# Two decoder layers on one core: the turns of the mixers' three chains in another order

## The chip, the cores and the metric

The kernel runs on one core of a Trainium2 chip. The metric is device microseconds of one execution. Five engines work side by side, each in the order of its own queue: PE (matrix products and transposes), DVE (VectorE), ACT (ScalarE), POOL (GpSimd) and SP, which here issues DMAs. A wait between engines is a wait for a semaphore.

## The reference

Two layers of a hybrid decoder trunk run on 512 tokens of width 1024, in f32. Each layer is a SwiGLU block, a token mixing block, a second SwiGLU block and a gated embedding, each with a norm ahead and a norm behind. The change touches only token mixing:

```
h = pre(x) @ W_in, columns split into attention | mLSTM | RWKV-7
y_attn  = sliding_window_gqa(q, k, v, sinks)            # 8 query heads, blocks of 128 queries x 256 keys
y_mlstm = sigmoid(o_m) * norm(mlstm_chunkwise(q, k, v, i, f))   # 4 heads, a running state from chunk to chunk
y_rwkv  = norm(rwkv7_scan(r, decay, k, v, a, b)) * gate         # 4 heads, a running state from token to token
x = x + post(concat(y_attn, y_mlstm, y_rwkv) @ W_out)
```

`o_m` is itself a projection of `h`: 1024 columns in, 256 out.

## The kernel before

Weights and activations of the large products are split into a high and a low part, and each product is three matmuls (`mm3`, lines 169 to 171). ACT makes the high part of a weight (line 141), DVE or POOL the low part (line 142).

In `mix` the inputs of all three mixers are projected first, RWKV's score matrices are made, and then `weave` runs four chains in turns. Each chain is a Python generator, and one call of `run` lets it record its instructions up to its next `yield`. The chains are:

- **A**, attention: 8 units (a block of 128 queries times a group of 4 heads), in 9 turns. A unit makes the scores (`pS`, line 1337), their maximum on DVE (1341, 1343), the exponentials on ACT (1349), sums and scaling on DVE and POOL (1350 to 1356), transposes (`pT`, 1366) and the product with the values (`po`, 1372). The product of unit u is recorded after the scores of unit u+1.
- **R**, RWKV: `rwkv_solve` inverts triangular blocks in two halves (`pt0`, `pgi`, `pt1`, `pz`, line 1017, with DVE additions at 1027 to 1034; then `pwt`, 869, and `pzq`, 877). The first half takes 15 turns. `rwkv_scan` then makes 8 steps, each dependent on the state `st` of the one before (`pq` 909, DVE 913, `pst` 919 to 921, state 923 and 925, output `py` 929 to 932); the turns of the second half of the solve lie between the first four steps. After the fifth and the last step come a norm (956 to 961, with a power on POOL at 179) and the transposes and gate products of `rwkv_back` (`pyt` 968, `pgf` 972, DVE 976 and 977).
- **M**, mLSTM: 4 chunks of 128 tokens. A chunk makes a weight matrix (`pwt` 1149, exponentials 1154, mask on POOL 1156), products `pss` (1163), `pnum` (1176), `pint` (1182), a state update from `pc` (1195), then norm and gating (1210 to 1223, the power at 179 and the multiplication by the gate `ng` at 1223 on POOL) and, in its `back`, the transposes `pym` (1140). All its products go through two PSUM banks in turn.
- **P**, the output gate projection of mLSTM: `tm_proj` into `pog`, 96 matmuls that need only `xh`, `xl` and two weight blocks, then a sigmoid on ACT and a product with the norm's gain on POOL (`ng`, 1123 and 1124).

The string `PLAN` gives the order of the turns; a letter whose chain is done is skipped, and what is left at its end runs in the order A, P, R, M. Two rules bind it. M doesn't start before A has had 7 turns. And the mixers' output is written over `xh` and `xl`, which P reads: a turn of R or M that would write there first runs P to its end, and attention's output `yt` is split into `xh` and `xl` once A and P are both done.

The recorded order isn't the order in the queues. The program is built with a scheduler that takes instructions by readiness on its own model of time and by recorded order, so a change of `PLAN` moves instructions on every engine, and it settles in which order tiles get their buffers.

Behind `weave` come `out_proj` (products `y`, lines 169 to 171, with weights `wo` for the first half of the columns and `wot` for the second), whose first half splits its weights on POOL, and the FFN. The second half's weights lie in the storage that the mixers used, so their loads `wor` wait until that is free. Lines named here and in the profile are those of the kernel before; in the changed kernel every line behind `PLAN` has a number that is lower by one.

Of the kernel before, what the change touches and what calls it, by code (L numbers as in the profile page):

```python
# [36 lines left out]
OE = "0000"  # L37
END = "XN"
NFL = {1: 1, 2: NT}
PLAN = ("AAAPAAAAAAAAAAAAAAPRARPARPAARRAPPAPA"  # L40
        "RRPARRPRRRMMMMARRPRRARPRARMRAAAPRMAR")
for _n, _w in (("amask", 384), ("mk_m", 64), ("mk_n", 256), ("mk_r", 64), ("m1", 64), ("m2", 64), ("bones", 128),
               ("triu", 128), ("lmask", 128), ("sel", 128)):
    CONSTS[_n] = (NCONST, _w)
# [28 lines left out]
class Trunk:  # L73
# [579 lines left out]
    def weave(self, l):  # L653
# [9 lines left out]
        def run(c):  # L663
            if c in done:
                return
            if c in "RM" and held.pop(c, None) and "P" not in done:
                while "P" not in done:
                    run("P")
            while c == "M" and c not in cycles and "A" not in done and count["A"] < 7:
                run("A")  # L670
            count[c] += 1
            if c not in cycles:
                self.lanes(*lanes[c])
            else:
                self.main, self.aux, self.chain = cycles[c]
            r = next(chains[c], "end")
            cycles[c] = self.main, self.aux, self.chain
            if r == "back":
                held[c] = True
            if r == "end":  # L680
                done.add(c)
            if c in "AP" and "A" in done and "P" in done:
                for t, y in enumerate(self.ys):
                    ts = slice(t * 128, (t + 1) * 128)
                    self.split(self.yh[:, 0:4, ts], self.yl[:, 0:4, ts], y.rearrange("p (a i) -> p a i", a=4),
                               self.pl_(1))
                done.add("Y")

        for c in PLAN:
            run(c)  # L690
# [828 lines left out]
```

## Time and profile before

| | us |
|---|---|
| median of three runs | 2180.99 (2180.17 to 2182.21) |
| the profiled run | 2184.07 |
| its span | 2182.4 |
| PE busy | 2104.1 (96%) |
| DVE busy | 1719.7 (79%) |
| ACT busy | 1008.8 (46%) |
| POOL busy | 327.4 (15%) |

The profile is of one execution. PE is busy nearly all the time, but ends of matmuls are modelled, so a row of dependent small matmuls also shows as busy. Layer 1 is a repetition of layer 0, and its mixing stage comes 1081.9 us later.

### The profile page before, as it was taken

What the parts mean: (1) busy time and instruction counts of PE and PEld (TensorE: products, weight loads), DVE (VectorE), ACT (ScalarE), POOL (GpSimd) and SP (SyncE); (2) the same over time, 40 slices, a digit from 0 to 9 for tenths busy, and PEclk for the clock granted to TensorE, in tenths of its full rate; (3) what the DMA queues carried; (4) which work ended last, traced back from release to release, by engine and by line L of the source; (5) the groups of instructions that cost most, each with busy time, mean ns of one, the idle gap of its engine ahead of it and who ended that gap; (6) DMA issues with size and microseconds to landing.
All of it is one profiled execution on the core that took longest, in us unless ns stands there. A gap on an engine that the chain in (4) does not pass through costs nothing.

```text
span 2182.4 us, 39847 instructions
## 1 busy us (share of the span) xinstructions
PE 2104.1 (96%) x16256; PEld 1957.1 (90%) x16256; DVE 1719.7 (79%) x2886; ACT 1008.8 (46%) x1653; POOL 327.4 (15%) x424
## 2 busy tenths in 40 slices
PE   6999999999988999999979999999999989999998
PEld 6999999898767999999869999998887789999996
DVE  8999977655768999977689999775457689999774
ACT  5444434446545444434554444345465454444343
POOL 5000011032234000011330000110412330000121
PEclk9999999999999999999999999999999999999999
DMA  4223224321041222224313222242220413222241
GB/s 174 106 99 115 69 78 156 119 64 55 21 154 40 108 106 101 84 68 175 105 59 116 105 90 88 81 175 87 64 64 2 155 59 117 97 97 78 78 143 71
DMA packets 69799, 208.62 MB, mean 96 GB/s; under 512 B 15984, under 2 KB 17008, under 8 KB 69616
## 3 DMA queue, kind: packets, MB, share of 16 engines
q1 hardware_dynamic: 69328, 205.55, 27.0%
q8 instruction: 128, 2.10, 0.4%
q10 hardware_dynamic: 288, 0.52, 0.1%
q14 instruction: 55, 0.45, 0.1%
HBM read 199.23 MB, written 6.82 MB: 94 GB/s over the span
## 4 chain that ended last, share of the span: by engine, by line
PE 82%; DVE 8%; ACT 4%; DMA 2%; issue 2%; POOL 1%; SPq 0%; POOLq 0%; DVEq 0%; ACTq 0%
PE y L465 18%; PE p L170 13%; PE p L169 13%; PE p L171 13%; PE pkrv L171 1%; PE pkrv L170 1%; PE pkrv L169 1%; PE y L169 1%; PE y L170 1%; PE y L171 1%; DMA ws_r<-in_w_ffn_out 1%; DVE w L142 1%; PE pgt L171 1%; PE pgt L169 1%; PE pgt L170 1%
## 5 line engine op out<-in xcount | busy, mean ns | idle before, releaser
L171 PE MATMUL p<-xh,w 128*128 128x256 f32 x1408 | 399.6, 285 | 6.3 <-POOL w L142 6.3
L169 PE MATMUL p<-xh,w 128*128 128x256 f32 x1408 | 400.1, 286 | 4.7 <-DVE gate L369 2.1
L170 PE MATMUL p<-xl,w 128*128 128x256 f32 x1408 | 400.3, 285 | 0.2 <-DVE xl L142 0.2
L169 PE MATMUL p<-tx,w 128*128 128x256 f32 x1056 | 296.9, 284 | 11.3 <-ACT tx L141 10.8
L170 PE MATMUL p<-tx,w 128*128 128x256 f32 x1056 | 296.3, 284 | 11.2 <-DVE tx L142 11.2
L171 PE MATMUL p<-tx,w 128*128 128x256 f32 x1056 | 295.7, 283 | 0.0
L171 PEld LDWEIGHTS p<-xh,w 128*128 128x128 f32 x1408 | 270.4, 192 | 7.0 <-POOL w L142 7.0
L169 PEld LDWEIGHTS p<-xh,w 128*128 128x128 f32 x1408 | 270.4, 193 | 6.9 <-DVE gate L369 2.9
L170 PEld LDWEIGHTS p<-xl,w 128*128 128x128 f32 x1408 | 270.9, 192 | 0.9 <-DVE xl L142 0.8
L141 ACT ACTIVATE w<-ws 128x1024 fp32r<-128x1024 f32 x176 | 185.9, 1056 | 153.4 <-PE p L171 134.8
L142 DVE TENSOR_TENSOR w<-ws,w 128x1024 fp32r<-128x1024 f32 x176 | 223.2, 1269 | 18.4 <-ACT w L141 17.2
L169 PEld LDWEIGHTS p<-tx,w 128*128 128x128 f32 x1056 | 202.5, 192 | 13.3 <-ACT tx L141 12.1
L170 PEld LDWEIGHTS p<-tx,w 128*128 128x128 f32 x1056 | 202.7, 192 | 12.1 <-DVE tx L142 12.1
L171 PEld LDWEIGHTS p<-tx,w 128*128 128x128 f32 x1056 | 201.4, 192 | 0.0
L141 ACT ACTIVATE w<-wr 128x512 fp32r<-128x512 f32 (+1 forms) x176 | 148.3, 844 | 114.5 <-PE p L171 67.1
L465 PE MATMUL y<-wo,hq 128*128 128x256 f32 x1536 | 193.3, 283 | 0.0
L465 PEld LDWEIGHTS y<-wo,hq 128*128 128x128 f32 x1536 | 186.4, 190 | 0.8
L501 POOL TENSOR_TENSOR tb<-tb,ln_ffn_post 128x512 f32<-128x512 f32 x16 | 24.1, 1530 | 1082.6 <-ACT junk L198 1082.6
L465 PE MATMUL y<-ws_r,h 128*128 128x256 f32 x672 | 158.3, 379 | 0.4 <-DMA ws_r<-in_w_ffn_out 0.2
L142 DVE TENSOR_TENSOR w<-wr,w 128x512 fp32r<-128x512 f32 (+1 forms) x161 | 150.9, 940 | 5.3 <-ACT w L141 4.9
L465 PEld LDWEIGHTS y<-ws_r,h 128*128 128x128 f32 x672 | 121.2, 189 | 14.9 <-DMA ws_r<-in_w_ffn_out 1.2
L357 DVE TENSOR_TENSOR ws<-wr 128x1024 f32<-128x1024 f32 x88 | 115.0, 1307 | 5.6 <-DMA wr<-in_w_ffn_in 5.3
(426 smaller groups left out, 4675.7 us busy)
## 6 DMA issues: line engine op xcount, KB each, us to landing
wr<-in_w_ffn_in SPq DMA_DIRECT2D x176, 512.0 KB, 4.1
ws_r<-in_w_ffn_out SPq DMA_DIRECT2D x56, 512.0 KB, 3.3
wo_r<-in_w_ffn_out SPq DMA_DIRECT2D x32, 512.0 KB, 3.3
pkrv_r<-in_w_rw SPq DMA_DIRECT2D x16, 512.0 KB, 3.5
wpg_r<-in_w_ple_gate SPq DMA_DIRECT2D x16, 512.0 KB, 4.5
xd<-x SPq DMA_DIRECT2D x8, 512.0 KB, 2.7
x<-xd SPq DMA_DIRECT2D x8, 512.0 KB, 3.4
pq_r<-in_w_q SPq DMA_DIRECT2D x8, 512.0 KB, 3.5
```

The costliest lines, as they stand in the source:

```text
L141: self.nc.scalar.activation(hi, src, AF.Copy)
L142: (eng or self.nc.vector).tensor_tensor(lo, src, hi.bitcast(F32), ALU.subtract)
L169: mm(out, a[0], b[0], start=first, stop=False)
L170: mm(out, a[0], b[1], start=False, stop=False)
L171: mm(out, a[1], b[0], start=False, stop=last)
L357: v_.tensor_tensor(sx.rearrange("p (i c) -> p i c", i=2), r[:, :, lo], r[:, 1].rearrange("p (i c) -> p i c", i=2), ALU.add)
L465: nc.tensor.matmul(banks[n][:, u], x, y, start=n not in seen, stop=last and i == len(todo) - 1, skip_group_check=True)
L501: (g_ if not h or QL[0] == "1" else v_).tensor_tensor(tb, tb, gain[:, h * 512:h * 512 + 512], ALU.mult)
```

## The change

Only `PLAN` is another string. The new one is written as repeated letters: A has its nine turns first, then R has the 15 turns of its first solve, then M its first turn, then R the first step of the scan, and only then P. R and M follow in turns.

```diff
-PLAN = ("AAAPAAAAAAAAAAAAAAPRARPARPAARRAPPAPA"
-        "RRPARRPRRRMMMMARRPRRARPRARMRAAAPRMAR")
+PLAN = 9 * "A" + 15 * "R" + "M" + 4 * "R" + "PM" + 4 * "R" + "M" + 3 * "R" + "PM" + 5 * "R" + "MM" + 5 * "R" + "MMM" + 4 * "R" + "MMM"
```

On PE, in layer 0, the gate projection's matmuls (`pog`) stood behind the transposes `pT` of attention's second unit, with the first solve's products (`pt`) and other products between them. Before:

```order
L1366 MATMUL pT<-ident,arena 128x128 x4
L169 MATMUL pog<-pog,xh 128x256
...
L1017 MATMUL pt_6077<-arena 64x64 x7
L1372 MATMUL po<-arena 64x512
...
L171 MATMUL pog<-pog,xl 128x256
L1091 MATMUL pir<-ident,vg 4x128 x4
```

In the changed kernel the first of them stands behind the second solve (`pzq`) and ahead of the very last attention product (`po`), and from the twelfth on they are one block up to the scan's fifth step (`pst`, `py`):

```order
L876 MATMUL pzq<-x,arena 64x64 x13
L908 MATMUL pq<-st,arena 64x128 x2
L918 MATMUL pst<-st,ident 64x128
L1371 MATMUL po<-arena 64x512
L168 MATMUL pog<-pog,xh 128x256
...
L170 MATMUL pog<-pog,xl 128x256
L920 MATMUL pst<-arena_4155 64x64 x2
```

The projection has moved from the third attention unit to the end of the eighth.

On ACT, in layer 0, the gates (`ng`) stood ahead of attention's units three to eight and of all of mLSTM. Before:

```order
L141 ACTIVATE xh<-yt 128x4x128
L1107 ACT_TABLE_LOAD
L1107 ACTIVATE vg<-vg 128x16
L141 ACTIVATE wo<-wo_r 128x1024
L1123 ACT_TABLE_LOAD
L1123 ACTIVATE ng<-pog 128x256 x4
L141 ACTIVATE wo<-wo_r 128x1024
L1112 ACT_TABLE_LOAD
```

In the changed kernel they stand, with the conversions of attention's output (`xh<-yt`) and of two weights (`wo`), ahead of the scan's state update (`st`), and mLSTM's third chunk (`pwt`, line 1153 here) comes two scan steps later:

```order
L140 ACTIVATE xh<-yt 128x4x128 x3
L140 ACTIVATE wo<-wo_r 128x1024
L1122 ACT_TABLE_LOAD
L1122 ACTIVATE ng<-pog 128x256 x4
L140 ACTIVATE wo<-wo_r 128x1024
L924 ACTIVATE st<-pst,pl 64x64 x2
L931 ACTIVATE x<-py 128x128 x2
L924 ACTIVATE st<-pst,pl 64x64 x2
L140 ACTIVATE xh<-arena 128x256 x2
```

The scan's updates are now queued behind the gates.

On PE, at the end of the weave in layer 0, mLSTM's last chunk (`pnum`, `pint`) was interleaved with the scan's last step. Before:

```order
L1176 MATMUL pnum<-vg,arena 128x128 x3
L1182 MATMUL pint<-arena 128x130 x2
L931 MATMUL py<-arena_4155 64x64 x2
L929 MATMUL py<-st,arena 64x128
L931 MATMUL py<-arena_4155 64x64 x2
L1140 MATMUL pym<-ident,mg 128x128 x2
L169 MATMUL y_6815<-wo,xh 128x512
```

In the changed kernel the third and the fourth chunk follow each other behind the scan, with RWKV's last transposes (`pyt`, `pgf`) between them:

```order
L1175 MATMUL pnum<-vg,arena 128x128 x4
L1181 MATMUL pint<-arena 128x130 x2
L1194 MATMUL pc<-vg,mg 128x130 x2
L1139 MATMUL pym<-ident,mg 128x128 x2
L967 MATMUL pyt<-ident,x 128x128 x4
L971 MATMUL pgf<-xg,arena 128x256 x2
L1148 MATMUL pwt<-ident,vg 128x128 x4
L1162 MATMUL pss<-arena 128x128 x4
L1175 MATMUL pnum<-vg,arena 128x128 x4
L1181 MATMUL pint<-arena 128x130 x2
L1139 MATMUL pym<-ident,mg 128x128 x2
```

Nothing but the first output products (`y`) stands behind them.

## Rows read from the trace of the kernel before

**Rows 1.** The page's chain of work that ended last, by engine

```profile
PE 82%; DVE 8%; ACT 4%; DMA 2%; issue 2%; POOL 1%; SPq 0%; POOLq 0%; DVEq 0%; ACTq 0%
```

**Rows 2.** Windows: length, then busy us (instructions) by engine, PEclk, DMA, GB/s

```profile
528.40:544.60 16.20, 16.08 (x135) 14.55 (x135) 7.77 (x25) 10.37 (x21) 1.67 (x2) 1.00 0.20 63
544.60:611.50 66.90, 63.83 (x777) 47.20 (x776) 49.25 (x162) 34.59 (x107) 19.50 (x21) 1.00 0.06 18
611.50:633.60 22.10, 16.78 (x131) 13.01 (x131) 17.30 (x50) 8.53 (x23) 8.77 (x7) 1.00 0.14 49
633.60:675.00 41.40, 41.40 (x189) 34.19 (x190) 23.74 (x27) 19.85 (x40) 15.27 (x16) 1.00 0.46 178
...
1693.40:1715.50 22.10, 16.77 (x131) 13.01 (x131) 17.30 (x50) 8.53 (x23) 8.78 (x7) 1.00 0.15 48
```

**Rows 3.** Timeline of PE: start, us, engine line op, names; the last attention product

```profile
610.01 1.45 PE L1372 MATMUL po<-arena 128*64 128x512 f32 x3
```

**Rows 4.** Timelines of four engines: mLSTM's last chunk up to its last transposes

```profile
614.66 1.14 ACT L1154 ACTIVATE arena<-pwt,vg 128x128 f32<-128x128 f32 x4 [0.81 <-PE pwt L1149]
615.93 0.64 POOL L1156 TENSOR_SCALAR_AFFINE_SELECT arena<-arena 128x512 f32<-128x512 f32 x1 [7.97 <-ACT arena L1154]
618.92 0.74 DVE L1164 SCALAR_TENSOR_TENSOR arena<-pss,arena 128x256 f32<-128x256 f32 x2
620.46 0.94 PE L1176 MATMUL pnum<-vg,arena 128*128 128x128 f32 x6
621.23 0.61 PE L1182 MATMUL pint<-arena 128*128 128x130 f32 x4
626.40 2.35 POOL L142 TENSOR_TENSOR wo<-wo_r,wo 128x1024 fp32r<-128x1024 f32 x1
633.56 0.44 PE L1140 MATMUL pym<-ident,mg 128*128 128x128 f32 x2 [1.51 <-POOL mg L1223]
```

**Rows 5.** Waits of PE from 490 to 650: the longest

```profile
PE pyt L968 <- DVE x L961: 2.0, 1, 2.0
```

**Rows 6.** Timeline of PE: two matmuls of the gate projection

```profile
544.19 0.28 PE L170 MATMUL pog<-pog,xh 128*128 128x256 f32 x1
544.31 0.28 PE L171 MATMUL pog<-pog,xl 128*128 128x256 f32 x1
```

**Rows 7.** Timelines of PE and ACT: one step of RWKV's scan and the next's start

```profile
616.49 0.44 PE L909 MATMUL pq<-st,arena 128*64 128x128 f32 x4
...
618.36 0.40 PE L931 MATMUL py<-arena 128*64 128x64 f32 x4
619.10 0.51 ACT L925 ACTIVATE st<-pst,pl 64x64 f32<-64x64 f32 x2
619.87 0.32 PE L909 MATMUL pq<-st,arena 128*64 128x128 f32 x1
```

**Rows 8.** Lines from 528 to 634: attention's exponentials; busy us, mean ns, idle before

```profile
L1349 ACT ACTIVATE arena<-arena,mx 128x256 f32<-128x256 f32 x24 | 11.9, 497 | 9.0 <-DVE mx L1343 7.0 <-DVE vg L1115 2.0
```

**Rows 9.** Timeline of ACT at the end of the gate projection

```profile
542.96 1.06 ACT L141 ACTIVATE wo<-wo_r 128x1024 fp32r<-128x1024 f32 x1 [0.25 <-PE pog L171]
544.03 1.28 ACT L1123 ACT_TABLE_LOAD   x1
545.33 1.21 ACT L1123 ACTIVATE ng<-pog 128x256 f32<-128x256 f32 x4
546.40 1.08 ACT L141 ACTIVATE wo<-wo_r 128x1024 fp32r<-128x1024 f32 x1
```

**Rows 10.** Timelines of DVE and POOL: a DVE instruction beside a weight split

```profile
549.65 1.53 DVE L1343 SCALAR_TENSOR_TENSOR mx<-mx,ns 128x4 f32<-128x4 f32 x1
548.79 2.37 POOL L142 TENSOR_TENSOR wo<-wo_r,wo 128x1024 fp32r<-128x1024 f32 x1
```

**Rows 11.** Windows at the start of the second FFN block, layer 0

```profile
695.00:700.00 5.00, 1.88 (x9) 1.48 (x9) 5.00 (x4) 3.08 (x6) 4.77 (x3) 0.74 0.00 0
700.00:705.00 5.00, 5.00 (x28) 5.00 (x28) 3.88 (x6) 0.00 (x0) 0.00 (x0) 0.58 0.00 0
```

## Prediction

> **What bounds the kernel now.** I read the chain of waits first: 82% of it is PE [rows 1], so the reader is to take PE as the engine that sets the time, and to ask of the change only where PE gains or loses a wait. Then the busy time by stretch, in the part of each layer in which the three mixers are woven [rows 2]. There are four stretches in layer 0. From 528.4 to 544.6 PE runs mLSTM's output gate projection, `pog`, among the other chains. From 544.6 to 611.5 the attention finishes while RWKV's second solve and scan and mLSTM's chunks run beside it; PE shows 63.83 of 66.90 us busy and DVE 49.25, so this stretch is dense. From 611.5 to 633.6 the attention is gone, only the scan's and mLSTM's dependent chains are left, and PE is busy 16.78 of 22.10 us. From 633.6 on the output projection has everything it needs and PE has no idle time in 41.40 us. The last attention product is the row at 610.01, ending at 611.46 [rows 3], and the last transpose of mLSTM's output, `pym`, starts at 633.56 [rows 4]. Layer 1 repeats this 1081.9 us later with the same figures (the tail's last row of [rows 2]: 16.77 of 22.10), so I work out one layer and double it. The waits by engine say what ends the idle time of that tail: PE waits longest for the DVE multiply before RWKV's transposes, 2.0 us [rows 5]. The tail is chains, not matmuls.
>
> **The change part by part.** No instruction's work is added or removed; the list of turns alone changes. What matters on PE is where the 96 `pog` matmuls stand, since they depend on nothing in the chains and can fill any gap.
>
> *The filler leaves the lead.* Two `pog` matmuls start 0.12 us apart (544.19 and 544.31 in [rows 6]), so the projection is worth 96 x 0.12 = 11.5 us of PE, which before is spread over the first of the four stretches. Now all of it stands behind the last but one attention product. More goes behind the last one: mLSTM's third chunk up to its `pint`, the first `pym` and the second half of the scan's fifth step. A scan step issues for 2.3 us on PE (616.49 to the end of the `py` row, 618.76, in [rows 7]), so its half is 1.2; the chunk's largest group, `pnum`, takes 0.94 for six of its eight rows [rows 4], and it has three more groups. I estimate 5 us in all. If PE waited no longer in the lead than it does now, the last attention product would end at 611.5 - 11.5 - 5 = 595.0.
>
> It will wait longer. In the new order of PE, RWKV's `pwt` products come right behind the first solve, and each needs the solve's last DVE addition. On DVE that stands behind the softmax of the fourth attention unit, which waits for that unit's four exponentials (497 ns each, [rows 8]); on ACT those now stand behind three table loads (1.28 us each, the form of the row at 544.03 in [rows 9]) instead of two. Nothing independent is left in PE's order there. I make that wait 5 us, of which the same stretch already has about 2 as waits between the chains, so I add 3, between -5 (the chains pack closer than they do now) and +8. Attention's end: 598.
>
> *The projection itself.* 11 of the 96 matmuls stand ahead of the last attention product, so 85 x 0.12 = 10.2 us follow: `pog` ends at 608.2. Call this E.
>
> *The tail behind it.* This is the term that decides. Before, ACT's run of conversions and gates at `pog`'s end (from 542.96: weight conversion 1.06, table load 1.28, gates 1.21, weight conversion 1.08, [rows 9]) held up nothing that was late. Now the scan's state update is queued behind the same run and one more conversion of attention's output: about 0.6 + 1.06 + 1.28 + 1.21 + 1.08 + 0.5 for the update itself = 5.7 us, so the sixth step starts at E + 6. A step takes 3.4 us from one `pq` to the next (616.49 to 619.87, [rows 7]); with RWKV's first back transform between, the eighth starts at E + 14. mLSTM's third chunk has its exponentials queued on ACT behind the seventh step's update and a table load: they end at E + 16.6 (1.28 + 1.14, [rows 4, 9]). From the exponentials to the end of `pint` I count mask, product, `pnum` and `pint`, 0.64 + 0.74 + 0.94 + 0.61, some 3.3 with hand-overs [rows 4]: E + 20. The fourth chunk's first transpose stands behind RWKV's last transposes, which wait for the norm of the eighth step: E + 23. Its exponentials and the same 3.3 us bring `pint` to E + 27.5. From there to the last `pym` it took 11.7 us before (621.84 to 633.56, [rows 4]), of which some 4 were POOL's weight split (2.35) and a DVE queue of RWKV's last step, which now comes earlier: I take 7.5. Sum E + 35; in layer 1 the order puts the third chunk's exponentials ahead of the scan's updates, which saves about 3. I take 34 for both, between 26 and 41. Below 22.1 it can't be, since all that the tail holds now stays in it.
>
> The last `pym` then starts at 608.2 + 34 = 642.2, against 633.6: 8.6 us a layer, 17 us for two.
>
> *Other engines and queues.* On POOL two `wo` splits and the four gate products now stand in the tail, ahead of the mask of mLSTM's third chunk; a split is 2.37 us [rows 10] and a gate product has a quarter of its elements, so 7 us is my estimate for the six. They begin at about E + 2 and are over by E + 10, and the mask is ready for POOL only at E + 16.6: the scan hides them, and if it did not, one split, 2.4 us, would be late. On SP the `ln_mix_post` loads move behind four loads of `w_out` and six of FFN weights. They are first read when the first output tile is done, 96 - 18 matmuls after the last `pym`; hidden, with nothing to gain. On ACT and DVE two splits of `w_out`'s second half move ahead of the split of the last `pym`, and three of PE's matmuls that read them ahead of the `pym` itself. That adds a wait for a DMA that can start only when the arena is free; behind it are 18 matmuls that don't read mLSTM's last tile. I cost it at 0, at most 3.
>
> The profiled run was 2184.07 us (span 2182.4) and the three timed runs have their median at 2180.99. The sum is a difference, so I add it to the median: 2181 + 17 = **2198 us**.
>
> **A page against the trace.** In [rows 10] a DVE instruction on 128x4 elements takes 1.53 us while POOL splits a weight, and ends when POOL does (551.18 and 551.16). The Trainium skill, "SBUF — State Buffer", section "Who interferes with whom", states that DVE and GpSimd have one port pair in common, which the first holds for a whole instruction when the DVE instruction reads two inputs from SBUF. The trace agrees, with the 1.53 us. By that rule the four DVE conversions of attention's output, all with two SBUF inputs and now beside POOL's splits and gates, would each wait, and the tail would be longer by up to two splits.
>
> **The rivals.**
>
> *The lead packs tighter (not slower).* Place: from 528 to the last attention product. With attention first in every turn, its units, the solve and mLSTM's first two chunks could fill PE without `pog`. For it: the dense stretch has DVE at only 49 of 67 us [rows 2], so there is room. Against it: with DVE and PE waiting on each other in order, less independent work means more waits. Its price: the lead 4 us better than now instead of 3 worse, and a tail of 30, gives 591 + 10.2 + 30 = 631.2, 2.4 us a layer to the good: 2176. It decides if `pog` ends before 599.6 with a tail of 34, or the tail is under 25.4 with the lead as forecast. Chance 0.17.
>
> *The waits only change places (no change).* The tail's extra waits equal those saved ahead of it, as PE has the same matmuls in all. 2181; chance 0.09, and 0.01 of the others falls there too. Against it: that needs a lead nearly free of waits.
>
> *PE's clock falls in the thin tail, or POOL blocks DVE there (slower still).* Place: E to E + 34. At the start of the FFN PE's busy time falls to 1.88 of 5 us, and the granted clock is 0.74 there and 0.58 in the next 5 us, when PE is busy throughout [rows 11]; of the two levels, 2.4 and 1.2 GHz, it has the lower for most of that time, and about 2 us of work are lost in 5. The tail has about 20 us of matmuls in 34. If the output projection starts at such a clock, 3 us a layer are lost, and one blocked split adds 2.4: 17 + 11, so 2209. Against it: 76% busy in the tail of before left the clock at 1.00 [rows 2]. Chance 0.10.
>
> **How the numbers follow.** The forecast has 0.64. From the bounds, a layer goes from 608.2 - 8 + 26 = 626.2 (7.4 us better) to 608.2 + 5 + 41 + 3 = 657 (23 us worse); both ends at once are unlikely. I leave out the outer part on each side: 2175 to 2215, the likeliest case's own range being 2188 to 2210. Within 0.2%, 4.4 us, a measurement can't tell a change. Faster 0.16, same 0.10, slower 0.74: the first rival is nearly all the chance of faster, the forecast and the last rival nearly all of slower.
>
> **What would show it.** Right: `pog` in one block of some 12 us that ends at 604 to 612 in layer 0; the last `pym` 30 us or more behind it, with PE under 70% busy between; a PE wait of some us at RWKV's `pwt` before the block; each layer 5 to 12 us longer and nothing changed after the output projection begins. Wrong: the block ends before 600, or mLSTM's third chunk runs under the scan in both layers and the tail is 27 us; or the FFN behind it, whose instructions the scheduler also orders a little differently, moves by more than 3 us.

## The result, and the profile after

The changed kernel takes 2215.23 us (median of four runs, 2213.61 to 2221.49) against 2181.49 (2180.17 to 2182.21) for the kernel before: a ratio of 1.0161, interval 1.0143 to 1.0179, 34 us slower. The forecast was 2198, slower by 17. The direction holds, the size is half of what came.

The chain of waits still has PE as the engine that sets the time, with 2 points less of it and 1 point more each for DVE and DMA than in [rows 1]:

```profile
PE 80%; DVE 9%; ACT 4%; DMA 3%; issue 2%; POOL 1%; SPq 0%; DVEq 0%; POOLq 0%; ACTq 0%
```

Windows of the changed kernel, columns as in [rows 2]: of layer 0 the lead (what stands ahead of `pog`), `pog` itself, the tail up to the last `pym`, the output projection; the fifth row is layer 1's tail.

```profile
528.40:595.60 67.20, 64.27 (x751) 46.52 (x750) 49.34 (x172) 35.30 (x107) 12.01 (x13) 0.95 0.05 16
595.60:608.60 13.00, 13.00 (x101) 11.90 (x102) 3.80 (x7) 4.84 (x7) 0.71 (x1) 1.00 0.01 1
608.60:648.20 39.60, 31.54 (x193) 26.15 (x193) 21.13 (x60) 15.68 (x38) 16.47 (x16) 0.74 0.30 102
648.20:689.60 41.40, 41.18 (x190) 33.83 (x188) 21.02 (x26) 18.10 (x39) 16.48 (x16) 1.00 0.35 133
...
1714.70:1750.10 35.40, 28.26 (x208) 21.82 (x208) 22.13 (x62) 15.06 (x36) 16.85 (x15) 0.90 0.31 109
```

`pog` is one block that ends at 608.6. Behind it come 39.6 us until the last `pym` where the kernel before had 22.1 behind its last attention product [rows 2], with a granted clock of 0.74 instead of 1.00. So for a part of that tail PE has the lower of its two levels, 1.2 GHz, and the tail's last chunk shows it: `pnum` takes 2.05 us for eight matmuls and `pint` 1.07 for four, where [rows 4] have 0.94 for six and 0.61 for four. Timelines of PE and DVE, changed kernel:

```profile
636.34 2.05 PE L1175 MATMUL pnum<-vg,arena 128*128 128x128 f32 x8 [1.84 <-DVE arena L1163]
638.18 1.07 PE L1181 MATMUL pint<-arena 128*128 128x130 f32 x4
642.95 1.43 DVE L1219 TENSOR_SCALAR ss<-ss 128x4 f32<-128x4 f32 x1
647.16 0.39 PE L170 MATMUL y<-wo,xl 128*128 128x512 f32 x1
647.38 0.87 PE L168 MATMUL y<-wot,xh 128*128 128x512 f32 x3
648.09 0.38 PE L1139 MATMUL pym<-ident,mg 128*128 128x128 f32 x2
```

The last `pym` doesn't wait for its `mg`, which ends at 646.73. From 641.00 on PE makes 21 products `y` of the output projection that stand ahead of it in PE's queue (the last four are the rows at 647.16 and 647.38), and the first of them start 0.43 us apart, the later ones 0.23: the lower level and the higher. So the tail ends with PE's own work and not with a bare chain.

The longest waits of PE from 528 to 650, the answer to [rows 5]. The first is in the lead, in the solve's second level and not at `pwt`, where the prediction put it; the second is the scan's sixth step behind ACT's run at the end of `pog`.

```profile
PE pz L1016 <- DVE arena L1026: 2.3, 1, 2.3
PE pq L908 <- ACT st L924: 1.9, 1, 1.9
PE pnum L1175 <- DVE arena L1163: 1.8, 1, 1.8
```

**Where the time came.** This profile's span is 2219.8 us, 37.4 more than before's 2182.4. Counted by where each stage begins, 13.6 us are there when FFN2 of layer 0 begins, 3.4 more when its products `p` end, 3.0 more between there and the end of layer 1's projections for the mixers, then again 13.6 in layer 1's mixing and 3.6 in its FFN2, and 0.2 at the end. The 3.0 are mostly what runs differ by: PE's order there is that of the kernel before, and in experiment 7, where it is so too, the same stretch was 2.0 us longer than in the profile of before. The output projection itself is no longer than before (41.4 us from the last `pym` to FFN2's first product, 42.3 before). So there are two places: the weave, 13.6 us a layer where 8.6 were forecast, and FFN2, 3.5 a layer where nothing was.

FFN2 first. PE there waits for `tx`, which DVE makes from the transposes of the last block. Timeline of DVE in the kernel before, at the start of FFN2:

```profile
683.26 3.50 DVE L209 SCALAR_TENSOR_TENSOR xn<-x,r,ln_ffn_pre 128x512 f32<-128x512 f32 x2
...
688.97 2.79 DVE L142 TENSOR_TENSOR w<-ws,w 128x1024 fp32r<-128x1024 f32 x1
691.68 0.68 DVE L241 TENSOR_TENSOR xr<-xr,xtp 128x512 f32<-128x512 f32 x1
692.28 1.21 DVE L357 TENSOR_TENSOR ws<-wr 128x1024 f32<-128x1024 f32 x1
693.42 0.68 DVE L242 SCALAR_TENSOR_TENSOR tx<-xtp,xr 128x512 f32<-128x512 f32 x1
694.02 0.68 DVE L243 TENSOR_TENSOR tx<-xtp,tx 128x512 f32<-128x512 f32 x1
```

and in the changed kernel:

```profile
698.18 4.58 DVE L208 SCALAR_TENSOR_TENSOR xn<-x,r,ln_ffn_pre 128x512 f32<-128x512 f32 x2
...
704.96 1.70 DVE L141 TENSOR_TENSOR w<-ws,w 128x1024 fp32r<-128x1024 f32 x1
706.70 1.22 DVE L356 TENSOR_TENSOR ws<-wr 128x1024 f32<-128x1024 f32 x1
707.84 1.22 DVE L141 TENSOR_TENSOR w<-ws,w 128x1024 fp32r<-128x1024 f32 x1
708.97 0.68 DVE L240 TENSOR_TENSOR xr<-xr,xtp 128x512 f32<-128x512 f32 x1
...
710.17 0.68 DVE L241 SCALAR_TENSOR_TENSOR tx<-xtp,xr 128x512 f32<-128x512 f32 x1
710.77 0.68 DVE L242 TENSOR_TENSOR tx<-xtp,tx 128x512 f32<-128x512 f32 x1
```

Before, `xr` follows one split of a weight; now a `ws` and a second split stand ahead of it. Counted from FFN2's first product (676.0 and 689.6), the second `tx` behind `xr` starts at 18.0 us before and 21.2 now: 3.2 us, nearly all of FFN2's 3.4 (241.3 us from its first product to its last before, 244.7 now). The instruction `xn` ahead of it has grown from 3.50 to 4.58 us; beside it POOL has another split, moved by the scheduler. A pair like it with no split on POOL takes 1.42 in the same trace (690.22). The Trainium skill, "SBUF — State Buffer", section "Who interferes with whom", says that a DVE instruction with two inputs from SBUF shares a port pair with a GpSimd instruction that reads SBUF, and that the one that came first keeps it; the trace agrees, with 4.58 against 1.42.

Windows at the start of FFN2, the answer to [rows 11]: PE is idle longer, and the stretch at the lower level comes behind it as before.

```profile
709.00:714.00 5.00, 1.16 (x2) 0.58 (x2) 5.00 (x7) 2.79 (x7) 3.61 (x3) 0.66 0.00 0
714.00:719.00 5.00, 2.84 (x13) 2.85 (x14) 4.41 (x5) 1.20 (x3) 3.24 (x2) 0.50 0.00 0
```

### The profile page after: what moved, and what is told of

It reads as the page before. It is cut to its first block, busy times and chain, and to the rows that moved or that the text cites. A ratio compares the mean times of both kernels' runs of the same rounds, so it can differ in the third digit from the quotient of the medians.

```text
span 2219.8 us, 39865 instructions
## 1 busy us (share of the span) xinstructions
PE 2131.0 (96%) x16256; PEld 1974.9 (89%) x16256; DVE 1717.3 (77%) x2886; ACT 1008.9 (45%) x1653; POOL 331.4 (15%) x424
## 4 chain that ended last, share of the span: by engine, by line
PE 80%; DVE 9%; ACT 4%; DMA 3%; issue 2%; POOL 1%; SPq 0%; DVEq 0%; POOLq 0%; ACTq 0%
PE y L464 17%; PE p L169 13%; PE p L170 13%; PE p L168 13%; PE y L168 1%; PE pkrv L170 1%; PE pkrv L169 1%; PE pkrv L168 1%; PE y L169 1%; PE y L170 1%; DMA ws_r<-in_w_ffn_out 1%; DVE xn L208 1%; PE po L1371 1%; PE pgt L169 1%; PE pgt L170 1%
## 5 line engine op out<-in xcount | busy, mean ns | idle before, releaser
L168 PE MATMUL p<-tx,w 128*128 128x256 f32 x1056 | 298.3, 286 | 16.4 <-ACT tx L140 15.9
L141 DVE TENSOR_TENSOR w<-wr,w 128x1024 fp32r<-128x1024 f32 (+1 forms) x161 | 151.3, 942 | 5.1 <-ACT w L140 4.3
```

What stands on the lines that cost most here:

```text
L141: (eng or self.nc.vector).tensor_tensor(lo, src, hi.bitcast(F32), ALU.subtract)
L168: mm(out, a[0], b[0], start=first, stop=False)
```

## The experiments

Experiments 1, 3, 4, 6, 8 and 10 to 12 start from the changed kernel, the others from the kernel before; each diff is against that kernel, that of experiment 9 against experiment 7. Line numbers in these kernels are near those of the kernel before. Intervals are of the ratio to the kernel before. "E" is the end of `pog`, "FFN2's length" the time from its first product `p` to its last.

**1. The old place of P in the new order.**

```diff
-PLAN = 9 * "A" + 15 * "R" + "M" + 4 * "R" + "PM" + 4 * "R" + ...
+PLAN = "AAAPAAAAAAP" + 15 * "R" + "M" + 4 * "R" + "M" + 4 * "R" + ...
```

> The changed order of A, R and M with P's first turn back behind A's third and the second behind A's ninth, as before the change. Theory 1 (the place of the 96 `pog` matmuls is all: without them the lead has a gap on PE, and behind the last attention product nothing is left to lie beside the chains of R and M): the time goes back to 2181 within 8 us. Rival (what was lost comes of recording R's solve and M's chunks in other places): it stays at 2205 or above.

Measured: 2201.89 us, 1.0075 to 1.0113. Neither. The last `pym` of layer 0 is at 631.1, earlier than before, but the scan now ends behind it: its last `pq` comes at 630.7 (620.3 before), the last `pyt` at 645.1. FFN2 begins 6.4 us later than before and is 4.5 us longer. So the new turns of R and M cost time of their own, and once more FFN2 is longer.

**2. P alone moved late.**

```diff
-PLAN = ("AAAPAAAAAAAAAAAAAAPRARPARPAARRAPPAPA"
-        "RRPARRPRRRMMMMARRPRRARPRARMRAAAPRMAR")
+PLAN = 9 * "A" + 12 * "R" + "PPMMMM" + 7 * "R" + "MRRMR"
```

> The order of A, R and M of the kernel before, with P alone moved late, behind A's ninth turn and R's twelfth (`pog` then stands behind the last attention product but one). Theory 1 (the place of `pog` is all): 2208 to 2222, with the granted clock below 1.00 in the lead (0.7 to 0.9 about 538 to 548 us) and in the tail. Rival (the other turns lost the time): 2181 to 2190.

Measured: 2216.37 us, 1.0133 to 1.0167; clock 0.98 and 0.96 in the leads, 0.95 and 0.90 in the tails. The place of P alone, with what the scheduler makes of it, gives the whole loss of the changed kernel; that of experiment 1 doesn't add to it.

**3. Filler for the tail.**

```diff
+FD = (28,)
...
+    def filler(self, counts):
+        for n in counts:
+            ps = self.mm_tile("fil")
+            for i in range(n):
+                self.nc.tensor.matmul(ps[:, 0:128], self.ident, self.const("lmask"), start=True, stop=True)
+            yield
```

> The changed kernel with 28 idle matmuls (128x128 f32, of constants, about 0.22 us each, 6 us a layer) recorded behind everything else, so that they stand in PE's gaps behind `pog`. Theory 2 (about 4 us a layer of the loss in the tail is PE's own work at the lower clock): the granted clock of 608 to 640 us rises from 0.77 to 0.95 or more, `pnum` goes from 1.6 to 2.05 us back to about 0.95, the last `pym` comes 2 to 4 us earlier than 648.2, and the time is 2205 to 2211 though PE has more to do. Rival (the chain over DVE, ACT and POOL sets the tail, the clock only follows): the clock rises but the last `pym` stays within 1 us or moves later by what of the 6 us stands ahead of the chain's own matmuls, 2215 to 2227.

Measured: 2220.04 us, 1.0155 to 1.0185. The clock of the tail is back at 0.95, yet the tail is 37.9 us:

```profile
606.60:644.50 37.90, 31.95 (x249) 26.26 (x249) 20.94 (x59) 15.69 (x38) 16.87 (x16) 0.95 0.30 100
```

The fillers stood ahead of the scan's steps in PE's queue (last `pq` at E + 18.1 instead of E + 11.6). From that `pq` to the last `pym` it is 19.8 us, against 27.9 in the changed kernel's layer 0 at 0.74, but the way there is 6.4 longer, and the order of the chains changed with it, so the two parts can't be set against each other one by one. As a cure it fails; as a test of the clock it is mixed, since it delays the scan itself.

**4. Filler for the lead.**

```diff
             for zq, sq, t0, gm in grp:
-                v_.tensor_tensor(zq, zq, prod(gm, zq, "pz"), ALU.add)
+                v_.tensor_tensor(zq, zq, prod(gm, zq, "pz", 12 if lev and not q and zq is grp[0][0] else 0), ALU.add)
```

Here `prod` first makes that many idle matmuls.

> The changed kernel with 12 idle matmuls (2.6 us a layer) ahead of the `pz` product of R's first solve that waits 2.5 us for DVE. Theory 2 (the gap in the lead lets the clock fall, which costs 3 us in layer 0 and 6 in layer 1): the clock stays at 1.00 from 538 to 548 and from 1640 to 1660 us, layer 1's last `pog` comes 4 to 6 us earlier, and the time is 2206 to 2211. Rival (the lead is bound by DVE and the chain, the clock is a bystander): 2214 to 2222.

Measured: 2216.09 us, 1.0141 to 1.0175: the rival, by the time. Layer 1's lead was at 1.00 and took 84.1 us, but the profile of experiment 8 took 84.0 at 0.98 with no filler. It doesn't settle the question, since the scheduler changed the tails too: 34.8 us in layer 0 and 39.9 in layer 1.

**5. P in the middle of the attention.**

```diff
-PLAN = ("AAAPAAAAAAAAAAAAAAPRARPARPAARRAPPAPA"
-        "RRPARRPRRRMMMMARRPRRARPRARMRAAAPRMAR")
+PLAN = "AAAAAPAAAAP" + 12 * "R" + "MMMM" + 7 * "R" + "MRRMR"
```

> The order of A, R and M of the kernel before, with P's turns two units of attention later (behind A's fifth turn and its ninth), so that `pog` stands in the middle of the attention: neither in the lead, where it filled PE's gap, nor behind the last attention product. Theory 1 (two separate losses: the gap and the clock of the lead, some 2 to 6 us a layer, and the bare tail, some 8 a layer, of which only the first is left here): last `pym` of layer 0 at 636 to 640 and 2190 to 2200 in all, with layer 1's FFN2, whose DVE and POOL instructions stand in another order than in the kernel before, 3 to 5 us longer than layer 0's, which keeps that order. Rival (all comes from the gap in the lead and the clock behind it): 2205 or above. Second rival (all comes from the tail): 2181 to 2187.

Measured: 2204.49 us, 1.0091 to 1.0124, as a whole near the first rival; but the two layers differ, and layer 0 is the test that was wanted. Its windows (beginning of the lead, the next 20 us, the tail):

```profile
528.00:538.00 10.00, 6.93 (x127) 5.04 (x126) 6.73 (x28) 8.19 (x19) 1.04 (x1) 1.00 0.27 98
538.00:558.40 20.40, 20.40 (x210) 14.51 (x210) 15.82 (x53) 9.79 (x36) 3.45 (x5) 0.92 0.01 2
613.20:635.60 22.40, 17.21 (x125) 13.07 (x124) 16.99 (x48) 8.37 (x23) 8.69 (x7) 1.00 0.14 48
```

PE's gap in the lead is there (6.93 of 10 us busy), the clock falls behind it, and still the last `pym` is only 1.9 us later than before, because attention covers the chains until the tail is as short as before: 22.4 us, at 1.00. From the end of the projections (`pvif`) to FFN2's first product it is 2.7 us more than before. FFN2 begins in before's order and is 2.2 us shorter (239.1 us), so that layer 0 ends where it did before. In layer 1 the scheduler made another order out of the same turns (lead 94.4 us, output projection 50.6, FFN2 245.1 with `xr` behind `ws` and two splits, much as in the changed kernel), and all of the loss is there.

**6. DVE's order in FFN2 pinned in the changed kernel.**

```diff
+            if w == 2 and m == 1:
+                v_.tensor_copy(sx[:, 0:1], self.xr[:, 1, 0, 0:1])
             v_.tensor_tensor(sx.rearrange("p (i c) -> p i c", i=2), r[:, :, lo],
...
+            if w == 2 and m == 0:
+                q = self.wsp.tile([128, 2, 1024], F32R, tag="w", name="w63")
+                v_.tensor_copy(q[:, 1, 0:1], self.xr[:, 1, 0, 0:1])
+                self.split(q[:, 0], q[:, 1], sy)
...
```

> The changed kernel with DVE's order at the start of FFN2 pinned: two instructions that are no part of the sums (a copy of one column of `xr` into a tile that is then overwritten) make `ws` of the second unit and the split of `w63` of the first wait for the last block's `xr`, so that `xr` no longer stands behind them. Theory 3 (FFN2's 3.5 us a layer are DVE's and POOL's order there): from the first product of FFN2 to its last 1.2 to 2.4 us a layer less than in the changed kernel (244.7 us), the whole 2210 to 2213. Rival (FFN2 is longer by the lower clock after a thinner output projection, the order is no matter): no less than 244 us a layer, 2214 to 2218.

Measured: 2207.44 us, 1.0101 to 1.0131, 7.8 below the changed kernel, more than expected. FFN2 takes 240.0 and 241.2 us. Counted from its first product (688.5), the second `tx` starts at 18.4 us (the row at 706.93, timeline of DVE):

```profile
703.87 1.71 DVE L142 TENSOR_TENSOR w<-ws,w 128x1024 fp32r<-128x1024 f32 x1
705.51 0.67 DVE L241 TENSOR_TENSOR xr<-xr,xtp 128x512 f32<-128x512 f32 x1
706.32 0.69 DVE L242 SCALAR_TENSOR_TENSOR tx<-xtp,xr 128x512 f32<-128x512 f32 x1
706.93 0.68 DVE L243 TENSOR_TENSOR tx<-xtp,tx 128x512 f32<-128x512 f32 x1
```

Its tails, 39.9 and 34.8 us, are the changed kernel's. So FFN2's loss comes of the order on DVE, with the clock that goes along: 0.89 in the first 60 us of the changed kernel's FFN2, 0.94 and 0.91 here.

**7. The same pins in the kernel before**, with no other edit than that of experiment 6.

> The kernel before with the same two pins in FFN2. Theory 3: `ws` (1.21 us) no longer stands between `xr` and `tx` on DVE, so that `tx`, which PE waits for, comes 1.2 us earlier in each layer: 2178.5 to 2181. Rival (the first unit's `w63` is then late instead): 2182 to 2186.

Measured: 2180.84 us, 0.9983 to 1.0002, in the range expected, though the interval holds 1, so that a gain of the whole isn't shown. In the profile FFN2 takes 238.8 us in each layer instead of 241.3.

**8. The changed kernel once more**, with no edit.

> The changed kernel once more, with the same instructions, for a second profile. Theory 2 (the clock is a cost of its own, which differs from run to run): a layer whose tail has a granted clock of 0.9 or more has a tail of 34 to 36 us, one at 0.75 some 40, and a lead of 83 us at 0.96 and 87 at 0.92, in any layer. Rival (the chain sets the time and the clock only shows the waiting): 39.6 and 35.4 us for the tails of layers 0 and 1 again, whatever the clock.

Measured: 2212.51 us in one run, span 2210.5. Windows of layer 0's lead and tail, then layer 1's:

```profile
528.00:594.60 66.60, 62.58 (x756) 44.87 (x754) 49.99 (x175) 35.56 (x107) 12.01 (x13) 1.00 0.05 17
607.50:644.70 37.20, 28.86 (x195) 23.41 (x194) 20.72 (x60) 15.74 (x38) 16.52 (x16) 0.82 0.31 106
1624.70:1693.30 68.60, 64.32 (x741) 45.83 (x739) 49.77 (x173) 35.22 (x107) 12.08 (x13) 0.98 0.05 17
1706.30:1741.80 35.50, 28.52 (x206) 21.94 (x207) 22.07 (x62) 15.01 (x36) 16.83 (x15) 0.90 0.32 107
```

The same instructions, another clock: layer 0's tail is 37.2 us at 0.82 instead of 39.6 at 0.74, layer 1's 35.5 at 0.90 as in the first profile, and layer 1's lead (end of `pvif` to end of `pog`) 84.0 at 0.98 instead of 87.0 at 0.92. So the clock is a cost of its own: 2.4 us in layer 0's tail, 3.0 in layer 1's lead and 1.4 in layer 0's (83.3 and 81.9), 6.8 of the 9.3 us between the two spans. What counts is where in the chain the clock falls, not the mean over the tail: from E + 16 to E + 24 in layer 0, where the mLSTM's third chunk goes over into the fourth, the first profile has 0.57 and the second 1.00. Experiment 6, whose engines keep the same order there, has 0.50, and a tail of 39.9 us at a mean of 0.79. Nor is the clock the whole tail: at 0.90 layer 1's still has 35.5.

**9. Pins in all four FFNs of the kernel before.**

```diff
-            if w == 2 and m == 1:
+            if m == 1:
...
-            if w == 2 and m == 0:
+            if m == 0:
```

> The kernel before with the two pins in all four FFNs. In the kernel before, layer 1's FFN1 has on DVE the order that the changed kernel has in FFN2 (`ws` and two splits of weights between the last block's `xl` and its `tx`), and lasts 246.3 us from first product to last, FFN2 241.3. Theory 3 (that order costs 3 to 5 us wherever it stands): layer 1's FFN1 at 241 to 243 us, FFN2 at 238.8, layer 0's FFN1 unchanged, and 2173 to 2177 in all, 4 to 6 below the kernel with FFN2 alone pinned. Rival (FFN1 is longer for another reason): 2179 to 2182 as with FFN2 alone.

Measured: 2176.07 us, 0.9959 to 0.9982, faster than both kernels. Layer 1's FFN1 goes from 246.6 to 242.0 us: the kernel before had the costly order there all along.

**10. The `wo` splits of the changed kernel on DVE.**

```diff
-OW = "1111"
+OW = "0000"
```

> The changed kernel with the low parts of the output projection's first weights made on DVE instead of POOL (four splits a layer, 2.37 us each on POOL). Theory 4 (what the tail lost over the forecast is DVE held up beside POOL's splits, 1.43 us for an instruction of 0.1 us in the gating): the tail is 2 to 3 us shorter in each layer, 2208 to 2212. Theory 2 (it is the clock, and four more splits of about 1.2 us on DVE lie beside the waits): within 3 us of 2215. Rival (DVE is in the chain): 2218 to 2225.

Measured: 2197.97 us, 1.0052 to 1.0082: 17.3 below the changed kernel, more than any theory had. Theory 4 isn't the reason: the 1.43 us of `ss` (642.95) lie beside the products `y` that PE makes then. FFN2 comes out in the order of the kernel before (240.6 us in both layers), and the tails are 6.7 and 5.9 us shorter than in the first profile, at a higher clock:

```profile
608.00:640.90 32.90, 25.85 (x189) 20.76 (x190) 20.71 (x61) 13.86 (x37) 11.12 (x13) 0.90 0.29 97
1703.70:1733.20 29.50, 25.39 (x215) 20.34 (x215) 22.33 (x62) 12.31 (x32) 11.75 (x12) 0.94 0.17 54
```

Timeline of POOL behind `pog` in the changed kernel:

```profile
607.89 2.36 POOL L141 TENSOR_TENSOR wo<-wo_r,wo 128x1024 fp32r<-128x1024 f32 x1 [13.16 <-ACT wo L140]
610.21 2.42 POOL L1123 TENSOR_TENSOR ng<-ng,arena 128x256 f32<-128x256 f32 x4
612.59 2.36 POOL L141 TENSOR_TENSOR wo<-wo_r,wo 128x1024 fp32r<-128x1024 f32 x1
614.89 1.43 POOL L1222 TENSOR_TENSOR mg<-mg,ng 128x256 f32<-128x256 f32 x2
622.89 0.64 POOL L1155 TENSOR_SCALAR_AFFINE_SELECT arena<-arena 128x512 f32<-128x512 f32 x1 [6.57 <-ACT arena L1153]
```

and of POOL and PE without the splits:

```profile
608.98 1.82 POOL L1124 TENSOR_TENSOR ng<-ng,arena 128x256 f32<-128x256 f32 x3 [14.86 <-ACT ng L1123]
610.77 1.75 POOL L1223 TENSOR_TENSOR mg<-mg,ng 128x256 f32<-128x256 f32 x1
612.57 0.44 PE L1140 MATMUL pym<-ident,mg 128*128 128x128 f32 x2 [0.46 <-POOL mg L1223]
615.95 0.64 POOL L1156 TENSOR_SCALAR_AFFINE_SELECT arena<-arena 128x512 f32<-128x512 f32 x1 [2.16 <-ACT arena L1154]
```

Here PE waits for `mg` itself, which ends at E + 4.5: `pym` (the first chunk's transposes, recorded with the second chunk's turn) is at 612.57, E + 4.6, and the mask of the third chunk at 615.95. With the splits that `mg`, the first of the two in the row at 614.89, ends at 615.64 (E + 7.0), `pym` follows behind the seventh scan step at 619.04 (E + 10.4), and the mask comes at 622.89. Timeline of PE, changed kernel:

```profile
616.69 0.44 PE L908 MATMUL pq<-st,arena 128*64 128x128 f32 x4
...
619.04 0.44 PE L1139 MATMUL pym<-ident,mg 128*128 128x128 f32 x2
```

There PE doesn't wait for `mg`, which has been done for 3.4 us: the scheduler put `pym` behind the seventh scan step, where without the splits it stands inside the sixth. So the edit did two things: some 2.5 us are POOL's queue, and 3.4 are the order that the scheduler made with the splits in it.

**11 and 12. Two of the four splits at a time.**

```diff
-OW = "1111"
+OW = "0011"
```

> The changed kernel with the first two of the four `wo` splits of a layer on DVE, the other two left on POOL. E is the end of `pog`. Theory 5 (the two splits that POOL runs right at E stand in its queue ahead of mLSTM's `mg`, so the second chunk's `pym`, and behind it in PE's queue the third chunk's `pwt`, come 6 us late): the first `pym` behind E starts at E + 5 instead of E + 10.5, the last at E + 30 to E + 34; layer 1's FFN2, which has DVE's order of the kernel before, lasts 241 us, layer 0's, which has that of the changed kernel, 244.5; 2200 to 2204 in all. Rival (the split late in the tail, beside which DVE's `ss` took 1.42 us, did it): first `pym` at E + 10, last at E + 35 or later, 2209 to 2214.

```diff
-OW = "1111"
+OW = "1100"
```

> The reverse: the first two splits stay on POOL, the last two go to DVE. Theory 5: the first `pym` still at E + 10, the last at E + 35 to E + 38; FFN2, which has the order of the kernel before in both layers, 240.5 to 241.5 us; 2204 to 2209. Rival (the late split did it): the last `pym` at E + 30 to E + 33, 2197 to 2201.

Measured: 2206.43 us (1.0093 to 1.0121) and 2204.27 (1.0079 to 1.0111). Layer 0's tails, first without POOL's first two splits, then without its last two:

```profile
608.40:641.10 32.70, 25.81 (x191) 21.21 (x191) 20.93 (x60) 13.34 (x36) 13.61 (x14) 0.90 0.26 87
```

```profile
607.50:644.80 37.30, 28.92 (x193) 23.44 (x193) 20.68 (x61) 15.75 (x38) 14.16 (x15) 0.82 0.32 107
```

The first time lies 2 us above theory 5's range, the second in it. In layer 0 it is the first two: `pym` at E + 4.6 and the tail 32.7 without them, E + 10.6 and 37.3 with them, and the order on PE goes with it as in experiment 10. Layer 1 is another matter. There POOL's order has `mg` ahead of the first split, its first `pym` is at E + 1.5 to E + 2.4 in all of these kernels, and the last comes at E + 35.3 with four splits on POOL, 34.3 with the last two, 32.9 with the first two, 29.3 with none. There the late split costs too, against theory 5: with the last two alone on POOL, the way from the end of the last `pint` to `pym` is 12.4 us, with none 7.9. The 2.4 us gained without the last two are gained earlier, ahead of the place of the late split, so they are the order's. FFN2 takes 244.4 and 239.2 us (first kernel; costly order in layer 0 alone) and 238.9 and 240.7 (second; costly order in neither).

**13. The kernel before with all pins and `wo` on DVE**: the edits of experiments 9 and 10 together.

> The kernel before with the pins of all four FFNs and all `wo` splits on DVE, as a candidate that beats both. Theory 5 (a split on POOL, 2.35 us at 626.40 in the tail of the kernel before, holds up the gating of mLSTM's last chunk): the last `pym` 2 to 3 us earlier in each layer, 2170 to 2173. Rival (DVE, 79% busy, takes the four splits of 1.23 us into the chain): 2177 to 2182.

Measured: 2171.18 us, 0.9935 to 0.9962, the fastest of all. Its last `pym` is at 631.2 instead of 633.7, and from the start of the last attention product to there it is 19.0 us, where the kernel before has 22.8:

```profile
612.20:631.20 19.00, 17.16 (x135) 13.37 (x133) 14.73 (x48) 7.79 (x21) 5.93 (x6) 1.00 0.09 30
```

## Why the prediction was half right

*The lead and the projection: right in number.* The last attention product was forecast to end at 598 and ended at 598.2 (597.2 in the second profile), `pog` was forecast to end at 608.2 and ended at 608.6 (607.5). The make-up of the lead is in part luck. The one long wait, 2.3 us, is at `pz` and not at `pwt`, and from 528.4 to the end of that product PE is idle for 3.2 us before, 2.9 in the first profile and 4.0 in the second: at most 0.8 us were added where the sum has 3. The first profile has clock in their place, 0.73 from 538 to 548.

*The mechanism: right.* Attention goes ahead, `pog` stands behind it, and what follows are chains that little covers. Layer 0 of experiment 5 shows it from the other side: with `pog` out of the lead but the chains covered by attention, the mixing loses 2.7 us and not 14.

*The tail up to the fourth chunk: right by errors that cancel.* The scan's sixth step was put at E + 6 and came at E + 3.1 (611.66); the third chunk's exponentials were put at E + 16.6 and ended at E + 14.2, the fourth's transposes at E + 23 and came at E + 23.1. But they would have been earlier still without POOL's splits, which the prediction took as hidden: in experiment 10 the fourth's transposes are at E + 16.4.

*The term that was too small in the weave is the last chunk.* From the fourth chunk's transposes to the last `pym` the sum has 12 us, 4.5 up to the end of `pint` and 7.5 behind it. Layer 0 took 7.5 and 8.8, layer 1 9.9 and 8.2, in the second profile 7.4 and 8.7, 10.2 and 8.1; in experiment 10, without the splits, it is still 16.5 and 15.2 us in all. In layer 0 DVE converts RWKV's last output ahead of `arena`, for which `pnum` waits 1.8 us, `pnum` and `pint` run at the lower level, and the 21 products `y` make `pym` 1.4 us later than `mg`. The sum had only three of these products as new ahead of `pym`, at nothing.

*Also wrong is "the scan hides them"*, said of POOL's two `wo` splits and four gate products. It looked at the mask as the instruction behind them. The instruction behind them is `mg` of the first chunk, on which `pym` depends, and behind `pym` in PE's queue stands the third chunk's `pwt`. The mask came late at 622.89 with the splits, and so seemed covered. The prediction's price, one split of 2.4 us if the cover were gone, is too small as well: without the splits the tails are 32.9 and 29.5 us, with them 37.2 to 39.6 and 35.5, though part of that is the order that the scheduler made with the splits, and the clock. With them gone the mixing costs 7.5 us in layer 0 and 7.7 in layer 1, close to the 8.6 forecast, and the whole kernel, with FFN2's order restored along the way, takes 2198.0. That this is the forecast's number is luck: the forecast had the splits in.

*The step that failed behind the weave is "nothing changed after the output projection begins".* FFN2 was 3.4 and 3.6 us longer through an order on DVE that the scheduler chose anew. Pinning it gives 7.8 us back. The prediction named a move of the FFN by more than 3 us as what would make it wrong.

*The clock was right as a rival and belonged in the sum.* It had a chance of 0.10 as a case apart, with the 1.00 in the tail of before as the reason against. It came beside the forecast's mechanism, in the lead and the tail and not at the start of the output projection, which kept 1.00: 0.74 to 0.90 in the tails and 0.92 to 1.00 in the leads, with 6.8 us between two profiles of the same instructions. Not shown is what a tail at 1.00 would take, since the filler that raised the clock also delayed the scan. The conversions of attention's output, the other half of that rival, were not held up by POOL: each takes 0.69 us, as before, and layer 0's last starts at 606.90, ahead of the first split.

*The account.* In the second profile the changed kernel is 28.1 us above the profile of before. The chains without POOL's splits are 15.2 of it (experiment 10's 7.5 and 7.7, from the end of `pvif` to FFN2's first product), the splits with their order and clock 5.7 (the second profile has 10.2 and 10.7 there), FFN2 6.0 (3.4 and 2.6), other places 1.2. The medians lie 33.7 apart, mainly because before's profile was 2.6 us above its median and the median of the changed kernel is 2.7 above this run. So of the 17 us that the forecast missed, FFN2 and the splits are 12 and what the profiles lie off the medians some 5; the other places and the bare chains, 2 us cheaper than the forecast, nearly cancel.

## What to carry to other kernels

When an engine's instructions are called hidden, look at every instruction that stands behind them in that engine's queue and at what depends on it; the one that was looked at may be late because of them. A sum that comes out right halfway can still be wrong in its terms: check each against the trace, the last stage too, where work of the next stage may already stand ahead in the queue. Where a scheduler places instructions by its own times, a moved stage reorders the next one too: compare the order at its critical handover (here `xr` and `tx` on DVE), and pin it if it matters. Work that depends on nothing belongs where chains would be bare; here, moved from one gap to the next, it cost more than its own length (experiment 2: 33 us for two layers, where the prediction puts the projection at 11.5 a layer).

## What the runs showed of the hardware

Four runs of the changed kernel differed by 8 us (2211.6 to 2219.8 in span) with the mean granted clock between 0.982 and 0.977. The kernel before, whose profile has 1.00 through the weave, stayed within 6.6 us (2177.2 to 2183.8) over all its runs. The tail with 0.74 shows PE busy 31.54 of 39.60 us, the tail of before with 1.00 16.78 of 22.10 [rows 2]. Two copies of one column, 0.14 us each on DVE, were worth 2.5 to 4.7 us in an FFN that had the costly order or before's, by what they held back.
